# Six edits to the order of work in a two-layer hybrid trunk: SSD norms and transposes, Down's forms, plain rows, first keys

## The chip, the cores and the metric

One core of one Trainium2 chip runs the whole program. The metric is the device time of one execution in microseconds (us); lower is better. TensorE (PE) multiplies matrices and leaves its results in eight PSUM banks; VectorE (DVE), ScalarE (ACT) and GpSimd (POOL) work element by element; SyncE (SP) issues most of the DMAs.

## The reference

Batch 1, 1024 tokens behind 16 learned meta tokens (L = 1040), width 1024, float32, two layers. Layer 0 is a Mamba-2 SSD mixer (inner width 2048, 4 groups of 8 heads of 64, state 128) and layer 1 a stick-breaking attention (16 heads of 64) over shared keys and values; each is followed by a gated FFN (inner width 2816) with a causal convolution of three taps.

```python
for layer in range(2):
    if layer == 0:
        h = h + ssd_mixer(rmsnorm(h, ssd_norm), ...)        # z, x|B|C, dt = u @ w_in
    else:
        k, v = split(rmsnorm(h_after_layer_0, kv_norm) @ w_kv)
        q = rmsnorm(h, sb_norm) @ w_q
        h = h + stick_breaking_attention(q, k, v) @ w_o
    u = causal_conv(rmsnorm(h, ffn_norm) @ w_up) + b        # 3 taps
    gate, val = split(u, 2)
    h = h + (silu(gate) * val) @ w_down
out = rmsnorm(h, final_norm)[:, 16:]

# the SSD mixer, for each group g of 8 heads, in chunks, with state S
cb = C_chunk @ B_chunk.T
y  = (cb * exp(decay)) @ (x * dt) + exp(a_cs) * (C_chunk @ S) + d_skip * x
S  = S * exp(a_total) + B_chunk.T @ (exp(decay_to_end) * x * dt)
hg = y * silu(z);  hg = hg * rsqrt(mean(hg * hg over the group)) * gate_g;  out = hg @ w_out
```

## The kernel before

Activations stand with channels on partitions and tokens on columns. Every fp32 product is made of three matmuls of split operands (`mm3`, L184 to L186: high by high, low by high, high by low). A low part is made after its high part: ACT copies (the high part), then DVE or POOL subtracts (L97 on POOL for weights, four pieces of 128x256).

**SSD stage** (`mixer`, about 90 to 685 us). For each of four groups the input projection (`in_group`: x, B, C) and the gate projection with the group's RMS norm (`gate_group`, `gate_norm`) are given out as *tiles* by a generator, `stream`: one tile is 24 matmuls of up to 348 columns. The tiles of later work are laid between the SSD's nine chunks of 116 tokens: a chunk's `ssd_front` (c b, the transposes of x and of b), then its share of tiles, during which `ssd_decays` makes the decays D (eight DVE operations L611, an Exp on ACT L612) and E (POOL) of the next chunk, then `ssd_back` (new state S, then y). The four compute engines run this stage in the order of the code (`manual_schedule`); elsewhere the framework's scheduler sets the order. The gate's blocks are followed by a norm of three token tiles, `norm(j)`, called from `stream` ahead of tiles 1, 2 and 3 of the next block: square sums on PE (`ms`, L217), Ln and Exp on ACT, five DVE steps (L222 to L225, L558). PSUM has tags mm (2 banks), sm (3), lg (2), ex (1); cb, pb, ms and y are taken from sm in turn. Groups 0 to 3 give out 18, 30, 30 and 18 tiles, evenly over the nine chunks.

**Down projection** (`Down` of each FFN, about 1350 to 1595 and 2711 to 2965 us). Sixteen of the 22 row blocks go through a Strassen-Winograd scheme of seven products, in rounds of two sets. A product's operands are made by `operands`: a sum or difference of weight quarters (a *w form*) and of gated activations (a *b form*) on DVE (L1051 to L1063), copies on ACT, low parts `wl` on POOL and `gl` on DVE (L1070). PE's results are added into `acc` (L1118) on DVE. The remaining six row blocks are the *plain rows*: four token tiles j of 260 (256 in layer 1) columns, each in eight blocks f of 128 output rows, 18 matmuls each, in five PSUM banks in turn (`banks`), added to h by DVE (L416 in `accumulate`). Between these adds 28 `sums` (L1087) put the seven products together; each is tied behind the last L1118 add. `tokens(x)` loads and splits the activations of a token half (L1138).

**Attention** starts with the first pair's keys: `load` fetches w_kv (POOL scales it by the norm's gain, ACT and POOL split it), and `norm` gives the normalised tokens, with `rstd` as the last of its steps.

**Entry of an FFN** (`enter_ffn`): the last product of the layer before in four tiles, with the operands of both token halves made ahead.

Of the kernel before, what the change touches and what calls it, by code (L numbers as in the profile page):

```python
# [70 lines left out]
XB, SQD = 9, (1, 4, 7)  # L71
SCALE = 0.125
PIECE = 256

# [25 lines left out]
class Trunk:  # L100
# [161 lines left out]
    def norm(self, h, j, u):  # L262

        s0, n = TT[j]
        if u is None:
            u = [(self.Q("uh", F32R), self.Q("ul", F32R)) for _ in range(KD)] + [self.rp.tile([P, QW], F32, tag="r", name=self.nm("r"))]
        rows = [h[k][:, s0 : s0 + n] for k in range(KD)]
        for k in range(KD):
            self.parts(rows[k], u[k], s0, n, None, self.nc.gpsimd if (j, k) in LPOOL else self.nc.vector)
        self.rstd(self.square_sum(rows, n, D), n, D, u[KD][:, HALO + s0 : HALO + s0 + n], j == 0)  # L270
        return u
# [294 lines left out]
    def stream(self, blocks, w0=None):  # L566


        calls = {}
        todo = []  # L570
        for src, f in blocks:
            if src is None:
                for j in range(3):
                    calls[3 * len(todo) + 1 + j] = lambda f=f, j=j: f(j)
            else:
                todo.append((src, f))
        w = [w0 or self.load_w(todo[0][0], D)]
        for n in range(3 * len(todo)):
            i, j = divmod(n, 3)
            if j == 0:  # L580
                if i + 1 < len(todo):
                    w.append(self.load_w(todo[i + 1][0], D))
                cur = w.pop(0)
            if n in calls:
                calls.pop(n)()
            todo[i][1](cur, j)
            yield
        self.settle()
        for f in calls.values():
            f()  # L590
# [27 lines left out]
    def ssd_front(self, g, x, bt, ct, c, dk, pool):  # L618

        nc = self.nc  # L620
        h0 = GH * g
        tt = nc.vector.tensor_tensor
        t0, n = CH[c]
        cc = 3 * (c % 3) + c // 3
        e = t0 + n
        pcb = self.sm("cb")
        nc.tensor.matmul(pcb[:n, :n], bt[:, t0:e], ct[:, t0:e], start=True, stop=True)
        px = self.lg("px")
        for q in range(4):
# [6 lines left out]
        tt(dk, dk, cbm[:n, :n].unsqueeze(1).to_broadcast([n, GH, n]), op=ALU.mult)  # L636
        bk = xde = None
        if c < 8:
            pb = self.sm("pb")
            nc.tensor.transpose(pb[:n, :P], bt[:, t0:e], self.ident)  # L640
            bk = pool.tile([P, P], F32, tag="bk", name=self.nm("bk"), bufs=2)
            nc.scalar.activation(bk[:n], pb[:n, :P], AF.Copy)  # L642
# [34 lines left out]
    def mixer(self, mx):  # L677
# [5 lines left out]
        with self.tc.tile_pool(name="ssd", bufs=3) as pool:  # L683
# [10 lines left out]
            def gate(g):  # L694
                def norm(j):
                    self.gate_norm(g, rows[g], accs[g], j)
                    if j == 2 and g < 2:
                        yd[g] = self.spill(rows[g][:4], f"y{g}_d")
                return self.gate_group(u, g, rows[g], accs[g], later if g == 3 else lambda j, f: f()) + [(None, norm)]

# [9 lines left out]
            with self.tc.manual_schedule(engines={E.PE, E.DVE, E.Activation, E.Pool}):  # L710
                ahead = self.ssd_decays(0, rows[0][5], 0, pool)
                dk, ce = next(ahead)
                for g in range(GROUPS):
                    *x, bt, ct = rows[g]
                    tiles, given = (18, 30, 30, 18)[g], 0
                    state = None
                    for c in range(9):
                        for _ in ahead:
                            pass
                        ops = self.ssd_front(g, x, bt, ct, c, dk, pool)  # L720
                        now = dk, ce
                        for _ in range((tiles * (c + 1) + 8) // 9 - given):
                            next(work)
                            if given == (tiles * c + 8) // 9:
                                nxt = (g, ct, c + 1) if c < 8 else (g + 1, rows[g + 1][5], 0) if g < 3 else None
# [15 lines left out]
    def out_proj(self, hd, ys, yd, pool):  # L741
# [13 lines left out]
        ws = [self.load_wd(a["w_out"][12 + i], i < 2) for i in range(4)]  # L755
        return self.enter_ffn(0, h, [(ws, first), (ws, half(1))], pool)

# [4 lines left out]
    def enter_ffn(self, layer, h, last, pool):  # L762
# [8 lines left out]
        banks = cycle((self.mm, self.lg, self.ex, self.mm, self.lg))  # L771
        ms = {}

        def tile(j, work):
            ws, ops = last[j // 2]
            ms[j] = self.sm("ms")
# [47 lines left out]
        w0 = self.up_weights(layer, 0, pool)  # L824
        ws0 = next(w0)
        for j in (0, 1):
            tile(j, iter(()))
            factors(j)
        store(0)
# [176 lines left out]
    def down(self, layer, gd, hd, pool, after, each=None):  # L1006
# [14 lines left out]

        def behind_up(ins):

            behind(ins, self.last_up, "behind the up projection")

# [3 lines left out]
        class Set:  # L1029
# [16 lines left out]
            def operands(me, i):  # L1046
# [3 lines left out]
                a11, a12, a21, a22 = w[0, 0], w[0, 1], w[1, 0], w[1, 1]  # L1050
                if i == 7:  # L1051
                    behind_up(tt(a21, a11, a21, op=SUB))
                    behind_up(tt(b12, b22, b12, op=SUB))
                elif i == 6:
                    tt(a21, a22, a21, op=SUB)
                    tt(b11, b11, b12, op=ADD)
                elif i == 5:
                    tt(a11, a11, a21, op=ADD)
                    tt(b12, b22, b11, op=SUB)
                elif i == 3:  # L1060
                    tt(a21, a12, a21, op=SUB)
                elif i == 4:
                    tt(b11, b21, b11, op=SUB)  # L1063
                x, y = {1: (b11, a11), 7: (b12, a21), 6: (b11, a21), 5: (b12, a11), 3: (b22, a21), 4: (b11, a22), 2: (b21, a12)}[i]
# [4 lines left out]
                nc.scalar.activation(gh, x, AF.Copy)  # L1069
                tt(gl, x, gh.bitcast(F32), op=SUB)  # L1070
                return gh, gl, wh, wl
# [58 lines left out]
        def tokens(x):  # L1130

            us[x] = []
            for b in rows:
# [3 lines left out]
                nc.scalar.activation(hi, lo.bitcast(F32), AF.Copy)  # L1137
                tt(lo, lo.bitcast(F32), hi.bitcast(F32), op=SUB)  # L1138
                us[x].append((hi, lo))
# [14 lines left out]
        for m in range(0, len(plan), 2):  # L1154
# [11 lines left out]
            for x in range(2):  # L1166
# [3 lines left out]
                if last and i == 4 and not x:  # L1170
                    tokens(0)
                    weights(rows[1], *own())
                    weights(rows[2], *(self.Q(z, F32R)[:, :D] for z in ("wh", "wl")))
                    for b in rows[3:]:
                        weights(b, *common())
# [9 lines left out]
        for j in range(4):  # L1185
            out = h if j > 1 else h[:4] + h22
            for f in range(KD):
                self.accumulate(out, f, FN * j, FN, lambda i, f: (ws[i][0][:, f * P : f * P + P], ws[i][1][:, f * P : f * P + P]), us[j // 2], bank=next(banks), base=S * (j // 2))
                for _ in range(2 if j == 0 else 1):
# [13 lines left out]
    def heads(self, u, p, pool):  # L1203
# [4 lines left out]
        class Pair:  # L1208
# [4 lines left out]
            def load(me, kind):  # L1213

                src, gain = {"k": (a["w_kv"][p], "kv_norm"), "q": (a["w_q"][p], "sb_norm"), "v": (a["w_kv"][PAIRS + p], "kv_norm")}[kind]
                w32 = self.wp.tile([P, 1024], F32, tag="w32", name=self.nm("w32"))
                nc.sync.dma_start(w32, src)
                if kind == "k":
                    me.ks = [self.Q("k", F32R), self.Q("k", F32R)]
                elif kind == "v":  # L1220
                    me.v = pool.tile([P, 9, P], F32, tag="v", name=self.nm("v"), bufs=2)
# [162 lines left out]
    def attention(self, u, pool):  # L1384
# [30 lines left out]
        for kind, j in (("k", 0), ("q", 0), ("k", 1), ("q", 1)):  # L1415
            for h in range(2):
                for f in first.half(kind, j, h):
                    f()
        self.token_factors(u[KD], pool)
        for p in range(PAIRS):  # L1420
# [25 lines left out]
    def o_proj(self, hd, od, pool):  # L1446
# [26 lines left out]
        ws = [self.load_wd(a["w_o"][first - 2 + i], i < 2) for i in range(4)]  # L1473
        return self.enter_ffn(1, h, [(ws[2:], ops), (ws, [part(p, 1) for p in range(first - 2, PAIRS)])], pool)

# [84 lines left out]
    def run(self, ctx):  # L1560
# [4 lines left out]
        with tc.tile_pool(name="ff0", bufs=2) as pool:  # L1565
# [80 lines left out]
```

## Time and profile before

| | |
|---|---|
| median of 3 runs | 2968.37 us (2966.44 to 2968.71) |
| profiled execution | 2966.99 us, span 2965.3 us, granted clock 0.989 |
| PE busy | 2870.4 us (97%) |
| DVE, ACT, POOL busy | 2139.3 (72%), 1649.1 (56%), 1614.5 us (54%) |
| chain that ended last | PE 81%, DVE 9%, issue 3%, ACT, POOL and DMA 2% each |

How to read it: the span runs from the first to the last recorded instruction, the execution's time is a little longer. A row of the timeline has start, duration, engine, line, operation and, in brackets, the idle time of the engine in front of it and what ended that. Durations on PE overlap, since matmuls are pipelined: two starts tell the pace. In a table of windows the busy times of the engines are followed by the granted clock (1.00 is full).

### The profile page before, as it was taken

To read this page: it belongs to the slowest core of one execution; us is meant where nothing else is said; L and a number is where in the kernel's file an instruction comes from. 1 tells how busy PE (TensorE), PEld (TensorE's weight loads), DVE (VectorE), ACT (ScalarE), POOL (GpSimd) and SP (SyncE) were. 2 spreads that over 40 slices of the span, in tenths; PEclk is the share of its full clock that TensorE was granted. 3 is DMA by queue.
4 is the path that set the end of the run, shared out by engine and by line. 5 is a ranking of instruction groups with operands and counts; after the bars stand their busy time and mean duration, and the time that the engine had idled before them with its cause. 6 is when DMAs were issued, how large, how long until landed. Compare 5 with 4: busy or idle time off the path is not lost.

```text
span 2965.3 us, 58614 instructions
## 1 busy us (share of the span) xinstructions
PE 2870.4 (97%) x21863; PEld 2730.3 (92%) x21863; DVE 2139.3 (72%) x4026; ACT 1649.1 (56%) x3399; POOL 1614.5 (54%) x2434
## 2 busy tenths in 40 slices
PE   7999999989999999999999999999999999999999
PEld 5999898879998999999999999999798999998888
DVE  5685958885368676667775888888839766767676
ACT  4555545553246556555334888887736555655433
POOL 1264545562346887876753222222353888886871
PEclk9999999999999999999999999999999999999999
DMA  5242333323121222225232122222331222225321
GB/s 164 76 114 80 109 96 102 98 74 140 59 97 62 78 80 79 80 90 185 70 131 82 55 65 64 66 69 55 111 138 58 83 83 79 76 83 178 107 100 65
DMA packets 123421, 272.80 MB, mean 92 GB/s; under 512 B 13664, under 2 KB 53216, under 8 KB 123136
## 3 DMA queue, kind: packets, MB, share of 16 engines
q1 hardware_dynamic: 117760, 257.93, 26.9%
q10 hardware_dynamic: 4112, 6.56, 0.7%
q0 software_dynamic: 1264, 4.57, 0.4%
q8 instruction: 172, 2.82, 0.4%
q14 instruction: 113, 0.93, 0.1%
HBM read 200.89 MB, written 53.20 MB: 86 GB/s over the span
## 4 chain that ended last, share of the span: by engine, by line
PE 81%; DVE 9%; issue 3%; ACT 2%; POOL 2%; DMA 2%; SPq 0%; DVEq 0%; ACTq 0%; POOLq 0%
PE p L184 10%; PE p L185 10%; PE p L186 10%; PE acc L185 7%; PE acc L184 7%; PE acc L186 7%; PE pj L184 6%; PE pj L185 6%; PE pj L186 6%; PE po L1379 3%; PE lg L1338 2%; PE wT L1365 2%; POOL wl L97 1%; PE ms L844 1%; DVE D L611 1%
## 5 line engine op out<-in xcount | busy, mean ns | idle before, releaser
L97 POOL TENSOR_TENSOR wl<-w,wh 128x256 fp32r<-128x256 f32 x780 | 692.1, 917 | 459.0 <-ACT wh L177 294.2
L184 PE MATMUL pj<-uh,wh 128*128 128x348 f32 (+2 forms) x1536 | 505.0, 329 | 9.7 <-ACT bk L642 5.2
L185 PE MATMUL pj<-ul,wh 128*128 128x348 f32 (+2 forms) x1536 | 498.4, 325 | 0.0
L186 PE MATMUL pj<-uh,wl 128*128 128x348 f32 (+2 forms) x1536 | 495.7, 323 | 0.8 <-POOL wl L97 0.8
L184 PE MATMUL p<-bh,fh 128*128 128x262 f32 (+1 forms) x1408 | 401.1, 286 | 2.2 <-ACT fh L917 2.2
L185 PE MATMUL p<-bl,fh 128*128 128x262 f32 (+1 forms) x1408 | 400.9, 285 | 1.0 <-DVE bl L870 0.7
L186 PE MATMUL p<-bh,fl 128*128 128x262 f32 (+1 forms) x1408 | 400.2, 285 | 0.4 <-POOL fl L97 0.4
L97 POOL TENSOR_TENSOR fl<-x,fh 128x256 fp32r<-128x256 f32 x352 | 260.8, 772 | 165.4 <-ACT fh L917 113.5
L185 PE MATMUL p<-bl,wh 128*128 128x262 f32 (+1 forms) x1056 | 302.8, 287 | 6.2 <-DVE bl L870 6.1
L184 PE MATMUL p<-bh,wh 128*128 128x262 f32 (+1 forms) x1056 | 303.8, 288 | 5.0 <-ACT ft L965 4.1
L184 PEld LDWEIGHTS pj<-uh,wh 128*128 128x128 f32 x1536 | 291.7, 190 | 14.3 <-ACT bk L642 5.8
L186 PE MATMUL p<-bh,wl 128*128 128x262 f32 (+1 forms) x1056 | 302.8, 287 | 0.0
L186 PEld LDWEIGHTS pj<-uh,wl 128*128 128x128 f32 x1536 | 291.7, 190 | 2.1 <-POOL wl L97 1.3
L185 PEld LDWEIGHTS pj<-ul,wh 128*128 128x128 f32 x1536 | 292.1, 190 | 1.3 <-issue 0.5
L309 DVE SCALAR_TENSOR_TENSOR c<-p,params,c 128x260 f32<-128x260 f32 (+1 forms) x528 | 249.2, 480 | 53.9 <-ACT c L306 47.0
L185 PEld LDWEIGHTS p<-bl,fh 128*128 128x128 f32 x1408 | 268.3, 191 | 2.7 <-DVE bl L870 2.4
L184 PEld LDWEIGHTS p<-bh,fh 128*128 128x128 f32 x1408 | 268.0, 191 | 2.7 <-ACT fh L917 2.6
L186 PEld LDWEIGHTS p<-bh,fl 128*128 128x128 f32 x1408 | 267.4, 190 | 0.9 <-POOL fl L97 0.8
L965 ACT ACTIVATE ft<-p 128x262 f32<-128x262 f32 (+1 forms) x352 | 133.3, 382 | 180.3 <-DVE p L968 108.1
L184 PE MATMUL acc<-gh,wh 128*128 128x260 f32 (+1 forms) x672 | 214.2, 322 | 7.1 <-DVE h L1118 6.1
L185 PE MATMUL acc<-gl,wh 128*128 128x260 f32 (+1 forms) x672 | 216.1, 322 | 3.7 <-DVE gl L1070 3.7
L186 PE MATMUL acc<-gh,wl 128*128 128x260 f32 (+1 forms) x672 | 215.0, 321 | 0.0
(319 smaller groups left out, 7974.8 us busy)
## 6 DMA issues: line engine op xcount, KB each, us to landing
w<-in_w_up SPq DMA_DIRECT2D x88, 512.0 KB
w<-in_w_down SPq DMA_DIRECT2D x44, 512.0 KB
w<-in_w_in SPq DMA_DIRECT2D x40, 512.0 KB
E<-ea_d SPq DMA_DIRECT2D x32, 464.0 KB
D<-acs_d SPq DMA_DIRECT2D x32, 420.5 KB
g<-c SPq DMA_DIRECT2D x88, 130.0 KB
g<-c SPq DMA_DIRECT2D x88, 128.0 KB
b<-g SPq DMA_DIRECT2D x16, 520.0 KB
```

Source lines behind the costliest of these rows:

```text
L97: eng.tensor_tensor(out[:, c], x[:, c], y[:, c], op=op)
L184: mm(out, wh, uh, start=first, stop=False, skip_group_check=joins)
L185: mm(out, wh, ul, start=False, stop=False, skip_group_check=joins)
L186: mm(out, wl, uh, start=False, stop=last, skip_group_check=joins)
L309: nc.vector.scalar_tensor_tensor(out, ps[:, o + i : o + i + n], wcol(i), out, op0=ALU.mult, op1=ALU.add)
L611: nc.vector.tensor_scalar(dk[:, i], dk[:, i], self.cols[:n, 1, cc, h0 + i : h0 + i + 1], 0.0, op0=ALU.subtract, op1=ALU.min)
L844: self.nc.tensor.matmul(ms[:, :n], self.ones, q, start=f == 0, stop=f == KD - 1, skip_group_check=True)
L965: nc.scalar.activation(s[:, :N], ps[:, :N], AF.Copy)
L1338: nc.tensor.matmul(ps[:nt, :m], part[:, c0 : c0 + nt], ks[a][:, s0 : s0 + m], start=x == 0, stop=x == 1)
L1365: nc.tensor.transpose(pt[:ns, x * CB : x * CB + nt], bt[a][:nt, x * CB : x * CB + ns], self.ident[:nt, :nt])
L1379: nc.tensor.matmul(po[64 * a : 64 * a + 64, :nt], v[: CH[c][1], c, 64 * a : 64 * a + 64], wt[a][: CH[c][1], c, :nt], start=x == 0, stop=x ...
```

## The change

1. *b beside c b.* The transpose of a chunk's b goes into columns 128 to 256 of the bank of c b, ahead of the matmul of c b, rather than into a bank of its own (`pb`).
2. *Norms two tiles apart.* `norm(0..2)` of groups 0 to 2 are called ahead of tiles 0, 2 and 4 after the gate's last tile; those of group 3 stay at 1, 2, 3.
3. *Shares.* The tiles of each chunk stand in a table; group 0 has one tile ahead of its first front and fewer at the end, group 3 gives out 21 (3 are left for the end, not 6).
4. *Down's ties.* A w form is tied behind the low part two back, a b form behind the last one, in the order of DVE; low parts of the second token half are tied behind the adds of the first plain tile.
5. *Plain rows' first tile over eight banks,* row block by row block: for each of the six row blocks, all eight f; its eight adds (L1212 in the new numbering) come at the end, and the sums (now L1102) are tied behind them. The third plain row block's weights go to other buffers, so that one more is loaded ahead.
6. *First keys.* Their weights are loaded, scaled and split while the plain rows run; `rstd` of the last token tile is called behind the first key half. `enter_ffn` makes each half's operands when its tile comes.

```diff
+SHARES = (3,) + 7 * (2,) + (1,), 3 * (4, 3, 3), 3 * (4, 3, 3), (3,) + 6 * (2,) + (3, 3)
...
-            if src is None:
+            if isinstance(src, tuple):
                 for j in range(3):
-                    calls[3 * len(todo) + 1 + j] = lambda f=f, j=j: f(j)
+                    calls[3 * len(todo) + src[j]] = lambda f=f, j=j: f(j)
...
         pcb = self.sm("cb")
+        if c < 8:
+            nc.tensor.transpose(pcb[:n, P : 2 * P], bt[:, t0:e], self.ident)
...
-            pb = self.sm("pb")
-            nc.tensor.transpose(pb[:n, :P], bt[:, t0:e], self.ident)
...
-            nc.scalar.activation(bk[:n], pb[:n, :P], AF.Copy)
+            nc.scalar.activation(bk[:n], pcb[:n, P : 2 * P], AF.Copy)
...
-    ... + [(None, norm)]
+    ... + [((0, 2, 4) if g < 3 else (1, 2, 3), norm)]
...
+        def behind_low(ins, n):
+            if len(lows) >= n:
+                behind(ins, lows[-n], "behind the low part in front")
...
+                for x, n in ((a, 2), (b, 1)):
+                    if x:
+                        d = tt(*x[:3], op=x[3])
+                        behind_low(d, n)
...
-                tt(gl, x, gh.bitcast(F32), op=SUB)
+                lows.append(tt(gl, x, gh.bitcast(F32), op=SUB))
...
+                if x:
+                    behind(low, self.last_add, "behind the first tile")
...
+            wide_first = [bank("acc") for bank in kinds] if j == 0 else []
+            for i, (hi, lo) in enumerate(us[0] if j == 0 else ()):
+                for f, ps in enumerate(wide_first):
+                    wh, wl = (w[:, f * P : f * P + P] for w in ws[i])
+                    self.mm3(ps[:, :FN], wh, wl, hi[:, :FN], lo[:, :FN], i == 0, i == len(ws) - 1)
             for f in range(KD):
-                self.accumulate(out, f, FN * j, FN, ...)
+                if j == 0:
+                    self.last_add = tt(out[f][:, :FN], out[f][:, :FN], wide_first[f][:, :FN], op=ADD)
+                else:
+                    self.accumulate(out, f, FN * j, FN, ...)
                 for _ in range(2 if j == 0 else 1):
                     next(work, None)
...
+                if j == 1:
+                    self.first_key = self.load_w(self.a["w_kv"][0], D, self.par("kv_norm", 0, KD))
```

The order on PE where the eighth of nine chunks of group 3 begins, before (L627 is c b, L630 the transposes of x, L640 that of b, L217 a square sum `ms` of gate 2's norm, L184 to L186 the next tile):

```order
L627 MATMUL cb_6406<-xbc_5378,xbc_5222 116x116
L630 MATMUL px_6408<-ident,xbc_4535 116x128
L630 MATMUL px_6408<-ident,xbc_4737 116x128
L630 MATMUL px_6408<-ident,xbc_4900 116x128
L630 MATMUL px_6408<-ident,xbc_5063 116x128
L640 MATMUL pb_6418<-ident,xbc_5222 116x128
L217 MATMUL ms_6426<-z_5587,ones 128x348
L184 MATMUL pj_6439<-uh_135,wh_6061 128x344
```

The same on PE after (line numbers of the new file are higher by six or seven here):

```order
L634 MATMUL cb_6417<-ident,xbc_5198 116x128
L635 MATMUL cb_6417<-xbc_5354,xbc_5198 116x116
L638 MATMUL px_6420<-ident,xbc_4529 116x128
L638 MATMUL px_6420<-ident,xbc_4697 116x128
L638 MATMUL px_6420<-ident,xbc_4878 116x128
L638 MATMUL px_6420<-ident,xbc_5040 116x128
L185 MATMUL pj_6444<-uh_135,wh_6193 128x348
L186 MATMUL pj_6444<-ul_136,wh_6193 128x348
```

The transpose of b stands first and in the bank of c b, and no square sum follows the transposes: the one of gate 2 that stood here comes a tile earlier in the program, the next one a tile later, each between two tiles.

The order on DVE at the start of Down in layer 1, before (L1052 and L1053 are the w and b forms of product 7, for both sets, L1055 and L1056 those of product 6; a gl, L1070, is the low part that PE needs):

```order
L1052 TENSOR_TENSOR w_34518<-w_34498,w_34518 128x1024
L1053 TENSOR_TENSOR b_34514<-b_34510,b_34514 128x2x512
L1052 TENSOR_TENSOR w_34520<-w_34500,w_34520 128x1024
L1053 TENSOR_TENSOR b_34516<-b_34512,b_34516 128x2x512
L1056 TENSOR_TENSOR b_34494<-b_34494,b_34514 128x2x512
L1056 TENSOR_TENSOR b_34496<-b_34496,b_34516 128x2x512
L1055 TENSOR_TENSOR w_34518<-w_34522,w_34518 128x1024
L1070 TENSOR_TENSOR gl_34638<-b_34504,gh_34637 128x2x512
```

The same on DVE after (L1075 is any form, L1085 a gl, L1133 an add of a product):

```order
L1075 TENSOR_TENSOR w_34486<-w_34466,w_34486 128x1024
L1085 TENSOR_TENSOR gl_34606<-b_34472,gh_34605 128x2x512
L1075 TENSOR_TENSOR b_34482<-b_34478,b_34482 128x2x512
L1075 TENSOR_TENSOR w_34488<-w_34468,w_34488 128x1024
L1133 TENSOR_TENSOR h_34494<-h_34494,acc_34616 128x512
L1085 TENSOR_TENSOR gl_34647<-b_34482,gh_34646 128x2x512
L1075 TENSOR_TENSOR b_34484<-b_34480,b_34484 128x2x512
L1075 TENSOR_TENSOR w_34486<-w_34490,w_34486 128x1024
```

Seven forms stood ahead of the first low part; now it stands behind the first form, and the first add behind the third.

The order on DVE in the plain rows of layer 0, before (L1087 a sum, L1138 a low part of `tokens`, L416 an add of tile 0's block):

```order
L1087 TENSOR_TENSOR p_15274<-p_15274,p_15271 128x520
L1087 TENSOR_TENSOR p_15275<-p_15275,p_15272 128x520
L1087 TENSOR_TENSOR p_15275<-p_15275,p_15273 128x520
L1138 TENSOR_TENSOR g_17492<-g_17492 128x520
L1138 TENSOR_TENSOR g_17496<-g_17496 128x520
L416 TENSOR_TENSOR h_15262<-h_15262,acc_17308 128x260
L416 TENSOR_TENSOR h_15263<-h_15263,acc_17330 128x260
L1087 TENSOR_TENSOR h_15266<-h_15266,p_15274 128x520
```

The same on DVE after, where tile 1's first adds stand (L1102 a sum, L422 an add of a block of tile 1; the block acc_17476 is tile 1's first, acc_17560 its fifth):

```order
L1102 TENSOR_TENSOR h_15235<-h_15235,p_15242 128x520
L1102 TENSOR_TENSOR h_15234<-h_15234,p_15242 128x520
L422 TENSOR_TENSOR h_15230<-h_15230,acc_17476 128x260
L422 TENSOR_TENSOR h_2155_17077<-h_2155_17077,acc_17560 128x260
L1102 TENSOR_TENSOR h_15232<-h_15232,h_15236 128x520
L1102 TENSOR_TENSOR h_15236<-h_15236,p_15243 128x520
L1153 TENSOR_TENSOR g_17468<-g_17468 128x520
```

Before, eleven sums and two low parts stood in front of the first add of tile 0. After, the first add of tile 1 has eight adds of tile 0, twenty sums and four low parts of the second token half between the last product and itself; it is followed by two sums and a low part, where the rows end, and then by more of both.

More of the change, by code (lines that the diff above doesn't have):

```diff
@@ L269, in norm @@
             self.parts(rows[k], u[k], s0, n, None, self.nc.gpsimd if (j, k) in LPOOL else self.nc.vector)
-        self.rstd(self.square_sum(rows, n, D), n, D, u[KD][:, HALO + s0 : HALO + s0 + n], j == 0)
+        sums = self.square_sum(rows, n, D)
+        factors = lambda: self.rstd(sums, n, D, u[KD][:, HALO + s0 : HALO + s0 + n], j == 0)
+        if j < 2:
+            factors()
+        else:
+            self.late_factors = factors
         return u
@@ L714, in mixer @@
                     *x, bt, ct = rows[g]
-                    tiles, given = (18, 30, 30, 18)[g], 0
+                    share, given = SHARES[g], 0
                     state = None
                     for c in range(9):
+                        if g == c == 0:
+                            next(work)
+                            given = 1
                         for _ in ahead:
                             pass
+                        begun = False
                         ops = self.ssd_front(g, x, bt, ct, c, dk, pool)
                         now = dk, ce
-                        for _ in range((tiles * (c + 1) + 8) // 9 - given):
+                        for _ in range(sum(share[: c + 1]) - given):
                             next(work)
-                            if given == (tiles * c + 8) // 9:
+                            if not begun:
+                                begun = True
                                 nxt = (g, ct, c + 1) if c < 8 else (g + 1, rows[g + 1][5], 0) if g < 3 else None
@@ L1172, in down @@
                     weights(rows[1], *own())
-                    weights(rows[2], *(self.Q(z, F32R)[:, :D] for z in ("wh", "wl")))
-                    for b in rows[3:]:
+                    weights(rows[2], *(pool.tile([P, QW], F32R, tag="x32", name=self.nm(z))[:, :D] for z in ("wh", "wl")))
+                    weights(rows[3], *(self.Q(z, F32R)[:, :D] for z in ("wh", "wl")))
+                    for b in rows[4:]:
                         weights(b, *common())
@@ L1473, in o_proj @@
         ws = [self.load_wd(a["w_o"][first - 2 + i], i < 2) for i in range(4)]
-        return self.enter_ffn(1, h, [(ws[2:], ops), (ws, [part(p, 1) for p in range(first - 2, PAIRS)])], pool)
+        second = [part(p, 1) for p in range(first - 2, PAIRS)]
+        return self.enter_ffn(1, h, [(ws[2:], lambda: ops), (ws, lambda: second)], pool)
     def finish(self, h, j):
```

49 lines of the change are left out of this document (25 added, 24 removed).

## The prediction

> **What bounds the kernel now.** I read the page first, then the chain of waits of TensorE, then the timeline around each long wait, with the clock in windows.
>
> ```profile
> span 2965.3 us, 58614 instructions
> PE 2870.4 (97%) x21863; PEld 2730.3 (92%) x21863; DVE 2139.3 (72%) x4026; ACT 1649.1 (56%) x3399; POOL 1614.5 (54%) x2434
> PE ms L217 <- ACT bk L642: 7.6, 3, 6.4
> PE acc L184 <- DVE h L1118: 6.1, 2, 5.3
> PE pj L184 <- ACT bk L642: 5.2, 2, 2.7
> PE pb L640 <- DVE z L223: 4.8, 2, 2.4
> PE acc L184 <- DVE h L416: 4.4, 4, 1.6
> PE acc L185 <- DVE gl L1070: 3.7, 1, 3.7
> PE S L657 <- POOL xde L97: 3.2, 4, 1.9
> PE pj L184 <- ACT wh L1229: 2.5, 2, 1.7
> PE y L669 <- DVE D L636: 1.7, 1, 1.7
> ```
>
> TensorE (PE) is busy for 2870.4 of 2965.3 us, so all its gaps together are 95 us, and the matmul work is the same after the change. An edit can only win some of these gaps and the slow clock behind them, or open new ones. The waits above (total, times, longest) are those that the change is near: 39.2 us. The next rows price the slow clock.
>
> ```profile
> 630.90:641.10 10.20, 6.21 (x20) 5.72 (x21) 9.65 (x26) 4.66 (x6) 2.79 (x3) 0.50 0.01 3
> 1378.40:1381.80 3.40, 3.35 (x15) 3.38 (x16) 3.40 (x3) 0.37 (x1) 3.40 (x4) 0.50 0.02 5
> 1603.70:1607.10 3.40, 2.90 (x10) 2.91 (x11) 0.00 (x0) 0.00 (x0) 3.40 (x6) 0.50 0.01 2
> 2733.50:2736.90 3.40, 3.01 (x7) 2.43 (x8) 3.40 (x3) 0.00 (x0) 2.60 (x2) 0.50 0.02 5
> 2880.20:2883.70 3.50, 3.50 (x19) 3.50 (x19) 3.50 (x5) 0.63 (x1) 2.01 (x2) 0.51 0.02 5
> 634.89 1.53 PE L217 MATMUL ms<-z,ones 128*128 128x348 f32 x2 [6.36 <-ACT bk L642]
> 1378.45 0.56 PE L184 MATMUL acc<-gh,wh 128*128 128x260 f32 x1 [5.27 <-DVE h L1118]
> 1603.08 0.43 PE L184 MATMUL pj<-uh,wh 128*128 128x348 f32 x1 [1.72 <-ACT wh L1229]
> 2733.89 0.80 PE L185 MATMUL acc<-gl,wh 128*128 128x512 f32 x1 [3.69 <-DVE gl L1070]
> 2878.48 0.39 PE L184 MATMUL acc<-g,wh 128*128 128x256 f32 x1 [1.75 <-ACT wh L1126]
> ```
>
> The last figures of a window row are granted clock, DMA share and GB/s. After each of these stalls (in brackets) the clock stood at 0.50 or 0.51 for 3.4 us, three times that around 634.89. Half of 3.4 us is lost: **1.7 us per slow window**. The Trainium skill ("TensorE: Matmul & The Clock Gate", section "Why this matters for your kernels") allows gaps of up to about 3 us; the trace disagrees, with 0.51 after a stall of 1.75. By the page the slow windows at 1603.7 and 2880.2 would not be won, and the sum would be 3.4 us higher.
>
> **SSD, groups 0 to 2.** The b transpose in the bank of c b adds no matmul and takes away a bank of its own and its waits (pb, 4.8). Whether time is won depends on who paces.
>
> ```profile
> 285.00:345.00 60.00, 53.57 (x355) 48.88 (x354) 52.34 (x102) 32.03 (x45) 30.25 (x40) 0.91 0.36 108
> 443.00:505.00 62.00, 54.80 (x376) 49.93 (x375) 54.06 (x108) 34.29 (x48) 30.72 (x41) 0.97 0.35 105
> 454.46 0.93 DVE L547 TENSOR_TENSOR z<-z,z 128x344 f32<-128x344 f32 x1 [2.90 <-ACT z L541]
> 486.50 1.81 DVE L309 SCALAR_TENSOR_TENSOR xbc<-pj,params,xbc 128x348 f32<-128x348 f32 x3 [1.58 <-ACT xbc L306]
> 218.16 4.13 DVE L611 TENSOR_SCALAR D<-D,cols 112x112 f32<-112x112 f32 x8
> 224.58 1.08 DVE L636 TENSOR_TENSOR D<-D,cbm 112x896 f32<-112x896 f32 x1
> 229.92 0.33 PE L184 MATMUL pj<-uh,wh 128*128 128x348 f32 x1
> 230.09 0.32 PE L185 MATMUL pj<-ul,wh 128*128 128x348 f32 x1
> ```
>
> Where gates 0 and 1 are normed, VectorE (DVE) works 52.34 of 60 and 54.06 of 62 us, as much as PE: both engines form one chain, and PE's waits are mostly DVE's time. Moving the norms to tiles 0, 2 and 4 puts the first sum of squares one tile earlier on PE, while its input z is ready when it was. The two gaps of DVE (2.90 and 1.58) grow, since norm(0)'s table load and functions now sit before the next Sigmoid on ACT, and the spill of y on POOL now waits for the later last norm, with E and state queued behind it. One DVE gap more is the price: I take +2.0 for group 1 (0 to 3) and +2.6 for group 2 (0 to 5). Group 0 gets a tile more ahead of its first front and one fewer behind its last: D of the last chunk comes 7.5 us after its decays begin (218.16 to 225.66), and a tile is 24 matmuls of 0.16 us, 3.8. Two tiles covered that, one leaves about 2.5 to 3.7; one tile more at the start wins 1 to 1.5. I take +1 (-1 to +4).
>
> **SSD, group 3.** Here the extra tiles do cover: the wait of 6.36 has bk's copy behind D's Exp on ACT, and D behind the norm's last step on DVE; with ms two tiles apart and b in the bank of c b it has no place. Won: 6.4, the slow clock in the running part of its window (10.2 less the 4.0 of the stall, halved, 3.1), about 2 of S waiting for xde and 1.7 of y waiting for D: 13.2. The sixth chunk's S comes a tile sooner behind POOL, about 2.7 anew (from the S waits, up to 1.9 each, and a tile), and 1.5 goes to smaller ones. **-9** (-12 to -6).
>
> **Down's ties.** In layer 1 (Down from 2711) a gl waits behind seven forms, the last of them waiting for POOL: 3.69 + 1.7 lost. With forms and low parts in turn, gl stands second; I leave 1.4 of new small waits: **-4** (-5.5 to -2). In layer 0 PE waits 5.27 + 1.7 for an add behind such forms; then gl of product 2 waits for its copy on ACT, which has the layer's last copies in front, and I count two stalls of about 1.0 and 2.9 as staying, with a slow window in one case of two: 7.0 - 3.9 - 0.9 = 2.2, so **-2.2** (-6 to 0).
>
> **First keys.** Their weights are now scaled and split beside the plain rows: 1.72 + 1.7 go, and most of the 0.8 that L1229's wait has beside it; the gain of rstd and of smaller waits nearby is about 0.5, and POOL's other weights stay where they are. I take **-4** (-5.5 to -2). Their one load moves ahead on SP's queue, behind the loads of the plain rows, which it therefore doesn't delay. The late rstd stands behind the first key half, hidden by it. Lazy operands at the FFN entries leave the order nearly as it is: 0.
>
> **Plain rows.** Before, the 28 sums of the products (L1087) run while tile 0 is on PE, and its adds (L416) stand behind eleven of them.
>
> ```profile
> 1522.67 3.89 DVE L1087 TENSOR_TENSOR p<-p 128x520 f32<-128x520 f32 x4
> 1533.60 0.75 DVE L416 TENSOR_TENSOR h<-h,acc 128x260 f32<-128x260 f32 x2
> 1534.06 0.39 PE L184 MATMUL acc<-g,fh 128*128 128x260 f32 x1 [1.61 <-DVE h L416]
> 1540.49 1.30 DVE L1087 TENSOR_TENSOR h<-h,h 128x520 f32<-128x520 f32 x2
> 1541.71 0.41 DVE L416 TENSOR_TENSOR h<-h,acc 128x260 f32<-128x260 f32 x1
> 1542.05 1.30 DVE L1087 TENSOR_TENSOR h<-h,h 128x520 f32<-128x520 f32 x2
> 1524.82 4.63 POOL L97 TENSOR_TENSOR wl<-w,wh 128x256 fp32r<-128x256 f32 x4
> 1527.00 0.28 PE L185 MATMUL acc<-g,wh 128*128 128x260 f32 x1
> 1527.12 0.28 PE L186 MATMUL acc<-g,wl 128*128 128x260 f32 x1
> 2889.17 0.39 PE L184 MATMUL acc<-g,fh 128*128 128x256 f32 x1 [1.30 <-DVE h L416]
> ```
>
> Starts tell DVE's pace: two sums take 1541.71 - 1540.49 = 1.22, so **0.61 a sum**, an add 1542.05 - 1541.71 = 0.34. PE starts a matmul every 0.12: 18 for a block of 128 columns, 2.16, a tile of eight 17.3. The wait of 1.61 is the sixth block of tile 0: five banks go round, and its bank still held the first block, whose add at 1533.60 stood behind the sums.
>
> After, tile 0 goes row by row over eight banks, so no add can start before its last row, and every sum is tied behind an add of tile 0. Let tile 0 end at 0. DVE starts at -2.3 with eight adds (2.7), 20 sums (12.2) and four low parts of the second token half (2.4, taken at a sum's pace); only then comes the add of tile 1's first block, done at **+15.4**. This is the order shown above the prediction. PE starts tile 1 at once (its five banks are free by +3.5), reaches the block that needs this bank after five blocks, +10.8, and waits 4.6. It then runs that block to 17.6 and stands before a block of tile 2 whose bank waits for the fourth block's add, behind the two adds, six sums and low parts, another add, three sums and two adds: 15.4 + 0.3 + 3.7 + 0.3 + 1.8 + 0.7 = 22.2. It waits another 4.6. Then DVE waits for PE and the lag is gone. New: 9.2, and one slow window behind it, 1.7 (the one after the first stall runs out inside the second): 10.9.
>
> Gone in layer 0: 1.61 and about 0.7 of late weights: 10.9 - 2.3 = **+8.6** (+3 to +11). In layer 1, where tile and order are alike: 1.75, 1.30 and the slow window at 2880.2: 10.9 - 4.8 = 6.1, taken as **+6** (0 to +8). This failing cover is the largest term against the change.
>
> The sums now run clear of POOL. Beside wl (to 1529.45) four took 3.89, 0.97 each, against 0.61 alone. The Trainium skill ("SBUF — State Buffer", section "SBUF: two separate sides") says that a DVE operation with two SBUF inputs and a GpSimd operation reading SBUF exclude each other; the trace agrees, 0.97 to 0.61.
>
> **The sum.** +1.0 + 2.0 + 2.6 - 9.0 - 2.2 - 4.0 - 4.0 + 8.6 + 6.0 = +1.0 us. The profiled execution took 2966.99 (span 2965.3 and 1.7 around it), giving 2968.0; it lies 1.4 below the median of the runs (2968.37), whose lowest is 2966.44, so the same sum on the median would be 2969.4. I forecast **2968**: no change. The bounds of the nine terms, taken as independent, give about 8 each way: 2960 to 2976.
>
> **Rivals.**
> - *The adds come in time (0.16).* If DVE's sums are spread so that PE never meets the sixth bank, the plain rows lose none of 10.9 twice: 2968.0 - 21.8 = 2946. For it: the wait of 1.61 was short although eleven sums at up to 0.97 stood in front. Against: 24 operations at 0.61 need 14.6 us and PE gives 10.8.
> - *Slower: POOL beside the sums (0.12).* POOL now scales and halves the first keys' weights in layer 0. Its pieces have DVE's empty time from 1529 to 1536; if their data land later, the 24 operations run at 0.97, and PE's stall grows by 24 x 0.36 = 8.6: 2977. It decides at the start of POOL's scaling after tile 0's last row.
> - *Slower: the norms stall PE (0.10).* If ms(0) of gates 1 and 2 waits 4.5 us in the open with a slow window, and tile 14 starts that much later, groups 1 and 2 cost 12.4 and not 4.6: 2976.
> - *Group 3's ms still meets a full bank (0.10).* If bk's copy stays in front of its bank, -9 is 0: 2978.
>
> Forecast 0.52, of which 0.40 lies within 0.2% (5.9 us, about what a measurement of this kernel can tell), 0.06 on either side. With the first rival faster is 0.22, with the three others slower 0.36 (0.02 of theirs within): same 0.42. The range 2952 to 2982 leaves out most of the first rival (0.13) and the far ends of the others.
>
> **What would show it.** Right: in the profile after, two PE waits on an add of plain rows, 4 to 5 us each and a block apart, in both layers, each pair behind 20 sums on DVE; no wait of ms on bk above 3; the first DVE gap after norm(0) of gate 1 above 4 us; no stall above 2 us at Down's start in layer 1; attention's first keys without a wait on wh. Wrong: PE busy through tile 1 (first rival), sums at 0.97 behind tile 0 (second), or a total below 2952.

## The result and the profile after

The changed kernel takes 2960.4 us (median of 12 runs, 2958.07 to 2963.63) against 2967.35 for the kernel before (12 runs beside it, 2958.55 to 2973.41): ratio 0.9981, 95% interval 0.9971 to 0.9990. That is 3 to 9 us less, where the forecast counted up to 5.9 us either way as no change. The profiled execution of it has a span of 2958.1 us, 7.2 less than before.

The page after, and TensorE's longest waits that the change is near (total, times, longest):

```profile
PE 2863.3 (97%) x21863; PEld 2724.6 (92%) x21863; DVE 2123.8 (72%) x4026; ACT 1650.7 (56%) x3398; POOL 1613.2 (55%) x2434
PE acc L185 <- DVE h L422: 10.6, 4, 4.5
PE ms L218 <- DVE z L553: 9.6, 2, 4.9
PE S L663 <- POOL xde L98: 8.9, 6, 4.3
PE pj L185 <- DVE xbc L315: 6.9, 2, 3.9
PE acc L185 <- DVE h L1133: 3.1, 4, 1.1
PE pj L185 <- DVE qs L1318: 1.7, 1, 1.7
```

The waits on bk (7.6 and 5.2), on z for pb (4.8), on gl (3.7) and the long one on the products' add (6.1) are gone. In their place stand an add of plain rows (10.6), square sums that wait for z (9.6), and more of S waiting for xde (8.9 after 3.2). Seen from TensorE, the change took about 27 us of waits away and put about 27 back; what is won does not lie there. TensorE's gaps come to 94.8 us, as before (94.9), and its busy time is 7.1 us less for the same number of instructions. By the granted clock, 0.990 rather than 0.989, some 3 us of that is slow clock (an estimate, since these figures are rounded). The stages tell where, and one of those that won, the second FFN, is a place where no edit was to win anything.

How long each stage took, between the first matmuls of the stages in the two traces, and what the prediction's sum had for it:

| stage | before | after | difference | predicted |
|---|---|---|---|---|
| to the end of SSD group 0 | 228.6 | 227.7 | -0.9 | +1.0 |
| group 1 | 158.4 | 162.5 | +4.1 | +2.0 |
| group 2 | 159.0 | 160.9 | +1.9 | +2.6 |
| group 3 | 137.9 | 135.1 | -2.8 | -9.0 |
| out_proj, first FFN to Down | 666.1 | 665.7 | -0.4 | 0 |
| Down 0 before the plain rows | 170.8 | 166.0 | -4.8 | -2.2 |
| plain rows 0 | 75.4 | 79.0 | +3.6 | +8.6 |
| attention | 547.0 | 543.8 | -3.2 | -4.0 |
| second FFN to Down | 568.2 | 564.5 | -3.7 | 0 |
| Down 1 before the plain rows | 161.5 | 159.4 | -2.2 | -4.0 |
| plain rows 1 to the end | 84.8 | 85.9 | +1.1 | +6.0 |

The new waits, in the timeline of TensorE after (in brackets what it stood idle for); the last rows are the clock in windows behind two of them:

```profile
288.52 1.53 PE L218 MATMUL ms<-z,ones 128*128 128x348 f32 x2 [4.86 <-DVE z L553]
450.88 1.50 PE L218 MATMUL ms<-z,ones 128*128 128x348 f32 x2 [4.72 <-DVE z L553]
640.26 2.08 PE L663 MATMUL S<-xde,bk 116*128 116x512 f32 x2 [4.28 <-POOL xde L98]
1550.70 0.59 PE L185 MATMUL acc<-g,fh 128*128 128x260 f32 x1 [4.49 <-DVE h L422]
2897.00 0.58 PE L185 MATMUL acc<-g,fh 128*128 128x256 f32 x1 [4.40 <-DVE h L422]
1550.60:1557.00 6.40, 6.30 (x29) 6.30 (x30) 6.40 (x13) 1.37 (x3) 1.41 (x1) 0.51 0.16 58
2897.00:2902.20 5.20, 5.20 (x26) 5.20 (x27) 5.20 (x10) 0.83 (x2) 2.92 (x2) 0.55 0.00 2
```

The two stalls in the plain rows, one in each layer, are the first of the two that were predicted for each: 4.6 was worked out, 4.49 and 4.40 came, at the block that takes the bank of tile 1's first.

### The profile page after: what moved, and what is told of

Its sections match the earlier page's. It is cut to its first block, busy times and chain, and to the rows that moved or that the text cites. A ratio compares the mean times of both kernels' runs of the same rounds, so it can differ in the third digit from the quotient of the medians.

```text
span 2958.1 us, 58618 instructions
## 1 busy us (share of the span) xinstructions
PE 2863.3 (97%) x21863; PEld 2724.6 (92%) x21863; DVE 2123.8 (72%) x4026; ACT 1650.7 (56%) x3398; POOL 1613.2 (55%) x2434
## 5 line engine op out<-in xcount | busy, mean ns | idle before, releaser
L186 PE MATMUL pj<-ul,wh 128*128 128x348 f32 (+2 forms) x1536 | 497.1, 324 | 0.0
L186 PE MATMUL p<-bl,fh 128*128 128x262 f32 (+1 forms) x1408 | 400.0, 285 | 0.1
L98 POOL TENSOR_TENSOR fl<-x,fh 128x256 fp32r<-128x256 f32 x352 | 260.0, 771 | 159.0 <-ACT fh L934 134.6
L186 PE MATMUL p<-bl,wh 128*128 128x262 f32 (+1 forms) x1056 | 301.1, 285 | 6.3 <-DVE bl L887 6.1
L186 PEld LDWEIGHTS pj<-ul,wh 128*128 128x128 f32 x1536 | 291.1, 190 | 1.4 <-issue 0.5
L186 PEld LDWEIGHTS p<-bl,fh 128*128 128x128 f32 x1408 | 267.6, 190 | 0.6 <-DVE bl L887 0.3
L186 PE MATMUL acc<-gl,wh 128*128 128x260 f32 (+1 forms) x672 | 213.9, 319 | 0.0
```

Of the source, the lines that this page charges most:

```text
L98: eng.tensor_tensor(out[:, c], x[:, c], y[:, c], op=op)
L186: mm(out, wh, ul, start=False, stop=False, skip_group_check=joins)
```

## The experiments

Each is the changed kernel with the edit shown, timed against the kernel before. Differences to the changed kernel are taken between ratios, times 2967 us; with intervals of 0.0009 to 0.0014 on either side of each ratio, less than 4 to 5 us is not told apart. What a trace shows is one execution, which can lie up to 4 us from the median.

**The SSD edits undone.** The diff takes back b's place, the norms' tiles and the shares.

```diff
-SHARES = (3,) + 7 * (2,) + (1,), 3 * (4, 3, 3), 3 * (4, 3, 3), (3,) + 6 * (2,) + (3, 3)
+SHARES = 9 * (2,), 3 * (4, 3, 3), 3 * (4, 3, 3), 9 * (2,)
...
-        + [((0, 2, 4) if g < 3 else (1, 2, 3), norm)]
+        + [((1, 2, 3), norm)]
```

> The changed kernel with the three edits of the SSD stage undone (b's transpose in its own bank, norms ahead of tiles 1, 2, 3, shares 18, 30, 30, 18), all else as changed. Theory A, read off the two traces by stage: the SSD edits cost 2.8 us in all (the first out_proj matmul starts 2.39 us later, the start 0.37 earlier), so 2960.4 - 2.8 = 2957.6, with the waits of ms on bk (6.4) and of pb on z back, and no wait of 4 to 5 on z. Theory B, my prediction's sum of the stage (-3.4): 2963.8.

Measured: 2955.63, ratio 0.9962 (0.9950 to 0.9975). Faster than the changed kernel by 5.6 us: the SSD edits cost time, as the stages say (theory A), and did not win the 3.4 of the prediction. In its trace the SSD stage is 3.8 us shorter than with the edits; another 3.1 went at the first FFN, where no SSD edit stands (see the operands made ahead, below). So what the SSD edits cost is nearer 2 to 4 us than 5.6. The waits of the kernel before are back in its trace (ms on bk 7.7 in all, 6.4 at the longest, pb on z 4.8).

**The norms one tile later.** `(0, 2, 4)` becomes `(1, 3, 5)`.

> The changed kernel with the norms of gates 0 to 2 ahead of tiles 1, 3 and 5 (not 0, 2 and 4), everything else as changed. Theory A: the 5.0 us that PE stands before the first square sum of gates 0 and 1, and the waits of 3 to 4 and of 2 behind it, come from calling the norm a tile too early; with a tile in front they go, up to the 8 us that groups 1 and 2 lost: 2952. Theory B: the stage is paced by the chain over DVE and ACT, so the waits move to other places and the time stays: 2958 to 2961.

Measured: 2955.73, ratio 0.9954 (0.9942 to 0.9967), 8 us below the changed kernel. The waits on z for `ms` fall from 9.6 to 1.8, but now `pj` waits for DVE's convolution twelve times (14.9 us in all, 6.9 in the changed kernel). Both theories have a part: groups 1 and 2 take 6.0 us less (158.8 and 158.6), and the waits that are left have moved.

**Only gate 2's norms two apart**, `(1, 2, 3)` for gates 0 and 1:

> The changed kernel with the norms of gates 0 and 1 ahead of tiles 1, 2 and 3 as before, and only gate 2's two apart (0, 2, 4). Theory A: groups 1 and 2 lose nothing then (they take 156.8 and 158.9 us from front to front with the SSD edits undone, 162.5 and 160.9 as changed): 2960.4 - 7.7 = 2952.7, with group 3's gain kept. Theory B, b's place and the shares cost the 7.7, not the norms: 2959 to 2961.

Measured: 2949.96, ratio 0.9936 (0.9924 to 0.9948), 13 us below. Group 1 takes 156.7 and group 2 156.7 us, against 162.5 and 160.9: 10.0 of it stand there. Theory A holds: norming gates 0 and 1 at 0, 2, 4 is what cost, and the share table and b's place did not. What TensorE still waits for there:

```profile
PE ms L218 <- DVE xbc L679: 4.7, 2, 3.1
PE ms L218 <- DVE z L224: 4.6, 2, 2.3
```

L224 is the step of the norm that `pb` waited for before (L223 there, 4.8 in two). With b in the bank of c b, that wait has moved to `ms`; it is not won.

**18 tiles in group 3**, `(3,) + 6 * (2,) + (3, 3)` becomes `9 * (2,)`:

> The changed kernel with 18 tiles, two a chunk, in group 3 (6 left for its end), not 21. Theory A: the three tiles won the waits of S for xde at the group's start (2.1) and of y for D at its end (1.9): they come back, 2960.4 + 4.0 = 2964.4. Theory B: those waits follow DVE's chain and the shares only move them: 2959 to 2962.

Measured: 2961.97, ratio 0.9982 (0.9973 to 0.9991): no difference, as theory B had it. In its trace the wait of S at the group's start is back, as theory A had it (1.93), but the longest one of S is 2.35, not 4.28: the shares move DVE's chain from one wait to the next.

**Plain rows block by block again.**

```diff
-            wide_first = [bank("acc") for bank in kinds] if j == 0 else []
...
-                if j == 0:
-                    self.last_add = tt(...)
+                self.accumulate(...)
```

The low parts of the second token half are not tied either; the weights' other buffers stay.

> The changed kernel with the first plain tile block by block over five banks again, and the sums and low parts tied as before. Theory A, by stage: the eight banks cost 3.6 us in layer 0 and 1.1 in layer 1, so 2960.4 - 4.7 = 2955.7, with the two PE waits of 4.5 on an add gone and waits of 1.3 to 1.8 back. Theory B, my prediction's two terms (8.6 and 6.0): 2945.8. Theory C, the eight banks win what they were meant to and the stall is covered elsewhere: 2960 or more.

Measured: 2959.98, ratio 0.9982 (0.9973 to 0.9990): no difference, so neither A nor B; it is theory C's figure. The two waits of 4.5 are gone. In layer 1 the plain rows take 84.8 us rather than 85.9; in layer 0 they take 81.6 rather than 79.0. There TensorE waits 8.45 us in tile 0 for an add of the products (L1133), which stands behind DVE's low part L1153, and this one, alone 0.6 us long, is held for 8.4. The profiled execution is 3.3 us above the median, so others may hold it less. The rows are of DVE, PE and POOL:

```profile
1520.09 8.37 DVE L1153 TENSOR_TENSOR g<-g 128x520 fp32r<-128x520 f32 x1 [4.44 <-ACT g L1152]
1528.72 0.69 DVE L1153 TENSOR_TENSOR g<-g 128x520 fp32r<-128x520 f32 x1
1530.13 0.58 PE L185 MATMUL acc<-g,fh 128*128 128x260 f32 x1 [8.45 <-DVE h L1133]
1512.21 8.39 POOL L98 TENSOR_TENSOR wl<-w,wh 128x256 fp32r<-128x256 f32 x12
1520.57 4.61 POOL L98 TENSOR_TENSOR w<-w,params 128x256 f32<-128x256 f32 x8
1525.14 2.77 POOL L98 TENSOR_TENSOR wl<-w,wh 128x256 fp32r<-128x256 f32 x4
```

POOL works through 24 pieces without a gap, 0.58 to 0.70 each, until 1527.91; DVE's operation ends at 1528.46. With eight banks DVE stands idle in that stretch (14.23 us, until tile 0's first add at 1532.89).

**The sums earlier.** They are tied behind the products' last add, so that they run while tile 0 is on PE.

```diff
+        products = self.last_add
         res, work = None, sums()
...
-  behind(tt(acc[x, f], acc[x, f], acc[y, f], op=ADD), self.last_add, ...)
+  behind(tt(acc[x, f], acc[x, f], acc[y, f], op=ADD), products, ...)
```

> The changed kernel with the sums of the seven products tied behind the last add of the products (fixed before tile 0), not behind tile 0's adds: most sums can run while tile 0 is on PE. Theory A: the wait of 4.5 us at tile 1's sixth block and the slow window behind it (1.7) go in both layers: 2960.4 - 12.4 = 2948.0; DVE reaches the first add of tile 1 about 8 us after tile 0's end, before PE needs its bank at 10.8. Theory B: the sums meet POOL's weight parts, take 0.97 rather than 0.61 and lag again, or PE waits for something else by then: 2955 to 2960.

Measured: 2946.45, ratio 0.9937 (0.9923 to 0.9950), 13 us below the changed kernel; 12.4 were worked out. The plain rows take 71.9 and 79.1 us rather than 79.0 and 85.9, and no wait for an add is left there. On DVE:

```profile
1516.41 4.83 DVE L1102 TENSOR_TENSOR p<-p 128x520 f32<-128x520 f32 x4
1542.87 0.41 DVE L422 TENSOR_TENSOR h<-h,acc 128x260 f32<-128x260 f32 x1
```

The sums beside POOL's row took up to 1.2 each, as theory B feared, and still the first add of tile 1 stands at 1542.87, not at 1550.23. That shows the 20 sums in front of this add as the cause of the 4.5 us and of the slow clock behind it.

**Down's ties undone** (the line `behind_low(d, n)` left out).

> The changed kernel without the ties of Down's forms to low parts (the tie of product 7 behind the up projection stays). Theory A, by stage: the ties won 4.8 us in layer 0 and 2.2 in layer 1, so 2960.4 + 7.0 = 2967.4, with PE waits of about 5.3 (add behind forms) and 3.7 (gl behind forms) back. Theory B: those waits went by another timing of DVE against POOL in that execution and not by the ties: 2960 to 2962, without these waits.

Measured: 2970.25, ratio 1.0014 (1.0005 to 1.0023), 10 us above. Both waits are back, by their places and causes:

```profile
1379.36 0.56 PE L185 MATMUL acc<-gh,wh 128*128 128x260 f32 x1 [6.06 <-DVE h L1132]
2735.01 0.79 PE L186 MATMUL acc<-gl,wh 128*128 128x512 f32 x1 [4.30 <-DVE gl L1084]
```

The ties are the change's largest gain, and theory A holds. In its trace Down takes 7.6 us more in layer 0 and 3.8 in layer 1 than with them.

**Operands made ahead at the FFNs' entry**, as before (`operands(1)` next to `operands(0)`).

> The changed kernel with both token halves' operands made ahead at the entry of the FFNs, as before. Theory A: the 3.6 us that went at the second FFN's start (and 1.5 at the first's) came from this edit; they come back: 2960.4 + 5.1 = 2965.5, with a PE wait above 2 about 63 us behind the start of each up projection. Theory B: they hang on whether one DVE operation is held for some 6 us by POOL's row of pieces in that execution, which this edit does not decide: 2960.4, within 2.

Measured: 2959.33, ratio 0.9972 (0.9961 to 0.9984): nothing lost (theory B), so the 3.7 us of the second FFN are not this edit's. What they were stands in the trace of before, on DVE, POOL and PE:

```profile
2316.37 6.50 DVE L968 TENSOR_TENSOR ft<-ft,ft 128x258 f32<-128x258 f32 x1
2315.62 2.83 POOL L97 TENSOR_TENSOR fl<-x,fh 128x256 fp32r<-128x256 f32 x4
2318.41 1.42 POOL L97 TENSOR_TENSOR wl<-w,wh 128x256 fp32r<-128x256 f32 x2
2319.80 1.42 POOL L97 TENSOR_TENSOR x<-w 128x256 f32<-128x256 f32 x2
2321.18 1.41 POOL L97 TENSOR_TENSOR x<-x,w 128x256 f32<-128x256 f32 x2
2323.83 0.56 PE L184 MATMUL p<-bh,wh 128*128 128x258 f32 x1 [2.20 <-ACT ft L965]
```

An operation of 0.8 us is held for 6.5, until POOL's row ends at 2322.59, and TensorE and the clock pay for it. In the trace after, and in that of this experiment, the same operation isn't held. Of the fourteen profiled executions it was held at this place in before's and in five others, whose entry is the changed one (3.7 to 6.7 us), and not in eight. The stage's time follows the length: 568.2 and 568.0 us with a hold of 6.5 and 6.65, 563.4 to 565.8 in the twelve with a shorter one or none. The same stands at the first FFN: 662.6 to 663.8 us in the three traces without a hold above 3 us (the SSD edits undone, this one and the first keys'), 664.6 to 667.3 in the others, which all have one of 5.1 to 6.5. So 2 to 3 us that these three traces gain over the changed kernel's stand there, and no edit of theirs is known to bring them.

**First keys without their place in the code**: the split and the last rstd stand in the code where they stood before.

> The changed kernel with the first keys' weights split at attention's start and the last rstd ahead of the first keys, as before. Theory A, by stage: the attention stage was 3.2 us shorter with the edit, 2963.6, and PE waits on wh at its start. Theory B: the same stage took 543.7 to 547.6 us in kernels that all have the edit, so it is worth 1 us or less: 2959 to 2961.4.

Measured: 2957.53, ratio 0.9974 (0.9965 to 0.9983): not told apart from the changed kernel, which is theory B, if anything a gain. With the edit TensorE waits 1.71 us on qs at 1611; without it no such wait stands at the stage's start. But no wait on wh is back either, and the split of the first keys' weights on ACT, in this run and in the kernel before, tells why:

```profile
1522.57 1.06 ACT L1252 ACTIVATE wh<-w 128x1024 fp32r<-128x1024 f32 x1 [2.30 <-POOL w L98]
1595.17 1.04 ACT L1229 ACTIVATE wh<-w 128x1024 fp32r<-128x1024 f32 x1
```

Here the split still runs beside the plain rows (1519.2 to 1598.4), though the code has it behind them. So this run takes back only the late rstd. It splits early as the changed kernel does, and what that is worth was not measured. What lets it run early without its line in the code is not shown; edit 5's other buffers for a row block's weights stayed in this run and may be it.

**Both gains together**, first with norms at 1, 3, 5, then with only gate 2's two apart, then with gate 2's at 0, 3, 6.

> The changed kernel with the sums tied behind the products' last add (as in e4_sums_early, 2946.45) and the norms of gates 0 to 2 ahead of tiles 1, 3 and 5. If both gains are of separate stages they add: 2946.4 - 8.0 = 2938.4 by theory A on the norms, 2946 by theory B.

Measured: 2945.74, ratio 0.9922 (0.9908 to 0.9935): 4 us below the early sums alone by the ratios, 1 by the medians, and not told apart from them.

> The changed kernel with both gains found: sums tied behind the products' last add (e4_sums_early, 14.0 below the changed kernel) and only gate 2's norms two apart (e6_norms_gate2_only, 10.4 below). Separate stages: 2960.4 - 24.4 = 2936.0. If either lives off the other's waits: 2940 to 2946.

Measured: 2942.58, ratio 0.9928 (0.9914 to 0.9942), 16 us below the changed kernel: less than the sum, by 6.6 us in the medians and 11 in the ratios. In the profiled execution a held operation at the second FFN again takes 3.5 of it (2.33 of TensorE's time and a slow window).

> As e11_best2, but gate 2's norms ahead of tiles 0, 3 and 6. Theory A: the wait of 4.4 us of S for xde in group 3 comes from norm(0)'s last DVE step (L564) standing ahead of the decays of the chunk, which each norm does once; another spacing moves it and does not remove it: 2936, within 3. Theory B: it comes from norm(1) being too near: 2932 or less, without a wait above 3 there.

Measured: **2940.43, ratio 0.9919 (0.9906 to 0.9932)**, the fastest, 18 us below the changed kernel, though not told apart from the two before it. The wait of S stays (4.88), as theory A has it, though the time is above its 2936, within 3. With norms at 1, 3, 5 it was gone (1.1 at the longest) and y waited 3.4 for D in its place. This trace also shows what the early sums risk, on DVE, POOL and PE:

```profile
1510.60 12.63 DVE L1102 TENSOR_TENSOR p<-p 128x520 f32<-128x520 f32 x4
1513.43 4.63 POOL L98 TENSOR_TENSOR w<-w,params 128x256 f32<-128x256 f32 x8
1518.00 2.84 POOL L98 TENSOR_TENSOR wl<-w,wh 128x256 fp32r<-128x256 f32 x4
1530.33 0.39 PE L185 MATMUL acc<-g,fh 128*128 128x260 f32 x1 [2.92 <-DVE h L1213]
```

Four sums take 12.63 us, 10.79 of it a single one, which ends half a us behind POOL's row (1520.84); 2.92 of it come through to TensorE.

## Why the prediction was right, and where it was not

The forecast was no change, 2968 within 2952 to 2982, and the time is 2960.4 with a ratio of 0.9981. The sum (+1.0) was 8 us too high, by terms that missed in both directions: by stage the plain rows were taken 9.9 too high and the FFNs 4.1, the SSD stage 5.8 too low. That the total came so near is in part luck.

**Plain rows, +14.6, measured +4.7 by stage.** The mechanism of the first stall was right and is shown by the early sums: no add before tile 0's last row, 20 sums and four low parts on DVE, a stall of 4.6 at tile 1's sixth block. The step that failed is the second stall of 4.6 at tile 2's first block. I took the banks to go round strictly, so that this block waited for the fourth block's add. The rows after, on DVE and PE:

```profile
1550.23 0.76 DVE L422 TENSOR_TENSOR h<-h,acc 128x260 f32<-128x260 f32 x2
1554.77 0.42 PE L185 MATMUL acc<-g,fh 128*128 128x260 f32 x1
1556.73 0.76 DVE L422 TENSOR_TENSOR h<-h,acc 128x260 f32<-128x260 f32 x2
```

Tile 2's first block starts at 1554.77, before the fourth block's add (in the pair at 1556.73): its bank is the one that the fifth block's add freed, the second of the pair at 1550.23. The order had that add right behind the first one, and I read past it. The slow clock was larger than the 1.7 taken: 0.51 for 6.4 us in layer 0 and 0.55 for 5.2 in layer 1, so about 3.1 and 2.3. Stall and clock make 7.6 and 6.7 us a layer, where 10.9 were worked out; the early sums took 7.1 and 6.8 off these stages.

**SSD, -3.4, measured +2.4 by stage and 5.6 by undoing (3.8 of it in these stages).** Groups 1 and 2 were forecast to lose for the reason that came (PE's first square sum a tile early, 4.86 and 4.72; 4.5 was worked out in the rival that put it in the open), but I had most of it absorbed by DVE's pace. Those stalls are the third rival's, and its 12.4 us for both groups is near what they cost: 13 us by the experiment with gate 2 alone, 10.0 of it in the two groups. Group 3, -9.0, came as -2.8. The waits of ms on bk (6.4) and of y for D (1.7) went as forecast. The step that failed is S waiting for xde: 2 were to go and 2.7 to come, and in this group it grew from 3.0 to 7.0, with one of 4.28. The slow clock stayed behind it: 3.1 were to be won, and TensorE's busy time in the group fell by 0.3 (126.87 to 126.55). The chain is the one that had stopped ms: norm(0)'s last DVE step in front of the decays, xdt behind them, then xde on POOL. What the edit took off one wait came back on the next in that chain. The chain is read from the order of the rows; that the wait can be moved is shown by the norms at 1, 3, 5.

**Down's ties, -6.2, measured -7.0 by stage and 10 by undoing.** Right in both places; I had left 1.0 and 2.9 of new stalls in layer 0, and none of them came at Down's start.

**First keys, -4, the stage measured -3.2.** The waits on wh went, and one on qs stands there. How much the early split won is not measured, since it ran early without its line in the code too. The wait of 1.72 was not for the keys' weights, as the prediction has it, but for the second split (ACT, 1601.97 to 1603.03), the queries', which came behind the keys'.

**FFN entries, 0.** Right as to the edit; the 3.7 us of the second FFN go with the hold of a DVE operation that this execution of the kernel before had.

The rivals: the adds that come in time, and group 3's ms on a full bank, did not come. POOL beside the sums was right as a mechanism and did not strike there, since POOL had ended at 1528.84, ahead of the sums at 1532.89; it struck where sums or low parts were moved into its row. The fourth rival's 2978 should read 2977 (2968 and 9).

## What to carry to other kernels

When an order changes, look for what now stands in front of the operation that frees a buffer, and count it in that engine's own pace: here 24 operations of 0.61 us against five blocks of 2.16 gave a stall to 0.2 us. Then read which buffer the waiting block takes out of the order itself, rather than by a rule of turns. Where two engines are paced by one chain, taking a wait away shows the next wait of that chain, so try the edit's parts alone. Here only Down's ties are shown to win as they stood; the norms of gates 0 and 1 lost, the plain rows, group 3's shares and the FFN entries won nothing that could be told apart, and b's place and the keys' early split were never measured alone.

## What the hardware showed

A DVE operation with two SBUF inputs can be held until POOL's whole row of pieces is through, not for one piece: 6.50 us (0.8 alone), 8.37 (0.6 alone) and 10.79 (0.6 alone), each ending within 0.6 us of the last piece. That POOL holds it is read from these ends; no run took POOL's row away. In other executions of like code the two alternate, 0.97 to 1.2 us an operation and 1.03 a piece. The Trainium skill ("SBUF — State Buffer", section "SBUF: two separate sides") has the loser blocked for an instruction; these rows go beyond that by eight pieces or more. Which of the two happens changed between executions of kernels that are alike there, and I found nothing in the traces that decides it.

A stall of TensorE just under 2 us may bring a slow window or not. The prediction's rows have two, 1.72 and 1.75, with a clock of 0.50 and 0.51 behind them; in the same trace the clock behind 1.83 (at 545.97), 1.92 (556.42) and 1.72 (659.42) stood at 1.00 for the next 7 us, and in the trace after so it did behind 1.71 (1611.35). So the 1.7 us for the slow window that the prediction gave each such stall is not owed by its length alone.
